# A mixture-of-experts stage: one expert goes from 128 slots with split weights to 64 slots with whole weights

## The chip, the cores and the metric

The kernel runs on one core of a Trainium2 chip. The metric is the device time of one launch in microseconds. The kernel before took 2102.27 us (median of three runs, 2098.06 to 2103.82).

## The reference

A two-layer model on 256 latent tokens and 256 context tokens, width 1024, float32. Layer 0 has neighbourhood attention, a state-space scan and a dense feed-forward; layer 1 has window attention and retention, and then, for the 256 latent tokens alone, a mixture of experts:

```
logits = h @ router                       # 256 x 8
top 2 experts of each token, softmax over the two -> gate
for e in 8 experts:                       # w1, w3: 1024 x 3584, w2: 3584 x 1024
    out += gate[:, e] * ((silu(h @ w1[e]) * (h @ w3[e])) @ w2[e])
```

The rest is `xl + g2 * out` and a last RMS norm. One expert's three matrices are 44 MB, all eight 352 MB, and each is read from HBM once. On its inputs the reference's router gives the eight experts 87, 39, 55, 145, 15, 52, 18 and 101 tokens.

## The kernel before

**Experts by rank.** Expert 0 is always position 0 (its loads start before the router is known). The other seven are sorted by their token counts into positions 1 to 7: here 145, 101, 55, 52, 39, 18 and 15 tokens. `CAPS` says how many slots each position has. Tokens are gathered into slots by a one-hot product (`gather_k`), and the outputs are scattered back by another (`comb` in `finish`). An expert with more tokens than slots would get a further whole pass in the `For_i` loop at the end (L1900).

**Two ways to multiply.** A *split* expert has 128 slots. Each weight tile (128 x 2048 float32, 1 MB) is split by ScalarE and VectorE into a high and a low float32r part (`split2`, L269 and L270); TensorE does three passes (L1554 to L1556) with all 128 columns of the array. A *whole* expert has 64 slots and uses the float32 tile as it is (`mmb`, L1551, and `stage_b`, L1763): the products of even and odd blocks stand side by side in the two 64-column halves of the array, and their partial sums are added later. Such a product shows as two records in the trace. Positions 0, 2 and 3 are split; 4 to 7 are whole; position 1 (192 slots) is split, with one block of 128 slots and one of 64 (L1558 and L1559, two passes).

**Chunks and their order.** Each expert is worked in 7 chunks of 512 hidden units. A chunk has 6 weight tiles: four of w1 and w3 (`stage_a`) and two of w2 (`stage_b`). The list `jobs` (L1447) sets the order: 7 chunks of position 0, 7 of 2, 7 of 3, then 28 of positions 4 to 7 with the 7 chunks of position 1 set between them. In the loop at L1867 `stage_a` of a chunk comes before `stage_b` of the chunk before; in the middle of `stage_a` the hidden values of the chunk before are transposed (`stage_t`). At each tile of `stage_a` one piece of waiting work is done (`fill`): a gather for a later expert (8 for each `prep_` call) or a `comb` of an expert that has ended (4 each).

**Weight tiles.** All weight DMAs go through SyncE's queue in the order of `plan`. Raw, high and low tiles share one tag of 11 buffers (`wtile`, NWT). `next_w` hands out the next tile; `prime` keeps 5 raw tiles fetched beyond those handed over and splits one tile ahead (AHEAD = 1). The tile framework places the instructions in its own order by priority, so a DMA can be issued as soon as a buffer is free.

**Sums.** The outputs of an expert are accumulated over its 7 chunks in the two PSUM banks of tag "mm". Position 1 cannot have these: its chunks go to banks of "ax" and "pt" and are added to `ysp` in SBUF by VectorE (L1858, L1860). `ysp` lies in the context half of `xT`, which nothing needs any more.

Of the kernel before, what the change touches and what calls it, by code (L numbers as in the profile page):

```python
# [10 lines left out]
F32 = mybir.dt.float32  # L11
# [7 lines left out]
P = 128  # L19
D = 1024  # L20
KD = 8
# [44 lines left out]
    return arrs, where  # L66


CAPS = (128, 192, 128, 128, 64, 64, 64, 64)
_CT, _CW = _const_tables()  # L70


# [95 lines left out]
def tile_backbone(ctx: ExitStack, tc: tile.TileContext, A, out, upto=99, dbg=None):  # L168
# [8 lines left out]
    AHEAD, LEAD, NWT, PRE, SPL = 1, 4, 11, (1, 3, 5, 7), (1, 3)  # L177
    LEADS = (6, 6, 6, 6, 5)
# [17 lines left out]
    def bank(tag="mm"):  # L196
        if turn and tag == "ax":
            turn.append(turn.pop(0))
            tag = turn[0]
        return ps[0].tile([P, 512], F32, tag=tag, name="bk_" + tag, bufs=NB[tag])  # L200
# [1199 lines left out]
            self.xt = xt  # L1400

    wpool, idx = [], []
    plan, loaded, ready, lead = [], [], [], [-1]

    def wtile(dt):
        return wpool[0].tile([P, 2048], dt, tag="w", name="w", bufs=NWT)
# [1 line left out]
    def load2(src, whole, parts=1):  # L1408
        raw = wtile(F32)
        dst, src = [a.rearrange("p (a b c) -> p a b c", a=2, b=parts) for a in (raw, src)]  # L1410
        for i in range(parts):
            nc.sync.dma_start(dst[:, :, i, :], src[:, :, i, :])
        return raw, whole
# [9 lines left out]
    def fetch():  # L1423
        loaded.append(plan.pop(0)())

    def prime():
        lead[0] += 1
        n = LEADS[min(lead[0], len(LEADS) - 1)]
        while plan and len(loaded) < n:
            fetch()  # L1430
        ready.append(split2(*loaded.pop(0), SPC if lead[0] < NSPC else 2048))

    def next_w():
        while len(ready) <= AHEAD and (loaded or plan):
            prime()
        return ready.pop(0)

    def w_dyn(r):
        return ((lambda c, i: A["m13"][bass.ds(r, 1), c, i].rearrange("o p k -> (o p) k")),
# [6 lines left out]

    jobs = []  # L1447
    job = 0
    for p in (0, 2, 3, 4, 5, 6, 7):
        for c in range(7):  # L1450
            jobs.append((p, c))
            if p >= 4:
                if job in (1, 5, 9, 13, 17, 20, 23):
                    jobs.append((1, sum(j[0] == 1 for j in jobs)))
                job += 1
    ws = {}

    def w_get(p):
        if p not in ws:
            ws[p] = w_of(p)  # L1460
        return ws[p]

    for n in range(len(jobs) + 1):
        if n < len(jobs):
            for i in range(4):
                plan.append(lambda p=jobs[n][0], c=jobs[n][1], i=i: load2(w_get(p)[0](c, i), p >= 4))
        if n:
            for q in range(2):
                plan.append(lambda p=jobs[n - 1][0], c=jobs[n - 1][1], q=q, n=n: load2(w_get(p)[1](c, q), p >= 4,
                                                                                 2 if n == len(jobs) else 1))  # L1470

    def moe(mp, dw, oh0):
        iota, iotd, rank8 = C("iota"), C("iotd"), C("rank8")
# [34 lines left out]
        def xg128():  # L1508
            return Pair(mp.tile([P, 2, KD, P], F32R, tag="xg", name="xg", bufs=4))
# [161 lines left out]
        def prep(specs, blocks, later):  # L1671
            oh = mk_oh(specs)
            ohT = mk_ohT(oh, specs)
            for k in range(KD):
                if later:
                    fills.append(lambda k=k: gather_k(oh, blocks, k))
                else:
                    gather_k(oh, blocks, k)
            return ohT
# [121 lines left out]
        def finish(src, gi, ohT, last=False):  # L1801
            for half in range(2):
                yh = mp.tile([P, 512], F32R, tag="yh", name="yh", bufs=2)
                yl = mp.tile([P, 512], F32R, tag="yl", name="yl", bufs=2)
                yhv, ylv = (yh, yl) if len(src[half].shape) == 2 else (two(yh), two(yl))
                S.activation(yhv, src[half], AF.Copy, scale=gsl[:, gi:gi + 1])
                V.scalar_tensor_tensor(ylv, src[half], gsl[:, gi:gi + 1], yhv.bitcast(F32),
                                       op0=ALU.mult, op1=ALU.subtract)

                def comb(m, yh=yh, yl=yl, half=half):  # L1810
                    pt = bank("ax" if last else "ada")
                    for i in range(2):
                        ms = slice((2 * m + i) * P, (2 * m + i + 1) * P)
                        o = pt[:, i * 256:i * 256 + 256]
                        T.matmul(o, yh[:, ms], ohT, start=True, stop=False)
                        T.matmul(o, yl[:, ms], ohT, start=False, stop=True)
                    for i in range(2):
                        resid(1, 5, 4 * half + 2 * m + i, pt[:, i * 256:i * 256 + 256], 1)
                        if last:
                            closing(4 * half + 2 * m + i)  # L1820

                for m in range(2):
                    fills.append(lambda m=m, comb=comb: comb(m))

        def spec(p, base=0.0, gi=None, io=iota):
            return (io, col(slp, p), base, col(gtp, p), p if gi is None else gi)


        def prep_b():
            xs[2], xs[3] = xg128(), xg128()  # L1830
            ohTs[2], ohTs[3] = prep([spec(2), spec(3)], [xs[2], xs[3]], True)

        def prep_c(a):
            t = mp.tile([P, 2, KD, 64], F32, tag="xg", name="xf", bufs=4)
# [8 lines left out]
        main = {}  # L1843

        def stage_2(p, c, gT):
            if p != 1:
                if c == 0:
                    main[p] = [[bank(), bank()]]
                stage_b(gT, main[p], c == 0, c == 6)
                if c == 6:  # L1850
                    finish(main[p][0], p, ohTs[p], p == 7)
                return
            acc = [[bank("ax"), bank("ax")] for _ in range(2)]
            stage_b(gT, acc, True, True)
            for b in range(2):
                for half in range(2):
                    if c == 0:
                        V.tensor_copy(ysp[b][half], two(acc[b][half]))  # L1858
                    else:
                        V.tensor_tensor(ysp[b][half], ysp[b][half], two(acc[b][half]), op=ALU.add)  # L1860
            if c == 6:
                finish(ysp[0], 1, ohTs[1])
                finish(ysp[1], 8, ohTs[8])

        prev = None
        gT = []
        for p, c in jobs:  # L1867
            if (p, c) == (0, 1):
                ohTs[0], = mk_ohT(oh0, [spec(0)])
                prep_b()  # L1870
            if (p, c) == (2, 1):
                prep_c(4)
            if (p, c) == (2, 3):
                prep_d()
            if (p, c) == (3, 1):
                prep_c(6)

            def mid():
                if prev is not None:
                    gT.append(stage_t(prev[1]))  # L1880

            gl = stage_a1(*a0) if prev is None else stage_a([xs[1], xs[8]] if p == 1 else [xs[p]], mid)
            if prev is not None:
                stage_2(*prev[0], gT.pop())
            prev = ((p, c), gl)
# [95 lines left out]
```

## Time and profile before

| | |
|---|---|
| Runs, median (range) | 2102.27 us (2098.06 to 2103.82) |
| Profiled execution | 2096.44 us, span 2094.7 us |
| PE / PEld / DVE / ACT busy | 97% / 69% / 61% / 43% of the span |
| Mean granted TensorE clock | 0.993 |
| Read from HBM | 493.40 MB, 236 GB/s over the span |

The busy time of PE is that of pipelined records whose ends are modelled. DMA is the mean busy share of the 16 DMA engines, GB/s what they moved. The experts begin at about half of the span, where GB/s rises above 300.

### The profile page before, as it was taken

To read this page: it belongs to the slowest core of one execution; us is meant where nothing else is said; L and a number is where in the kernel's file an instruction comes from. 1 tells how busy PE (TensorE), PEld (TensorE's weight loads), DVE (VectorE), ACT (ScalarE), POOL (GpSimd) and SP (SyncE) were. 2 spreads that over 40 slices of the span, in tenths; PEclk is the share of its full clock that TensorE was granted. 3 is DMA by queue.
4 is the path that set the end of the run, shared out by engine and by line. 5 is a ranking of instruction groups with operands and counts; after the bars stand their busy time and mean duration, and the time that the engine had idled before them with its cause. 6 is when DMAs were issued, how large, how long until landed. Compare 5 with 4: busy or idle time off the path is not lost. (4 is left out here: it accounts for less than half of the span.)

```text
span 2094.7 us, 26701 instructions
## 1 busy us (share of the span) xinstructions
PE 2026.0 (97%) x10170; PEld 1438.0 (69%) x10170; DVE 1288.0 (61%) x1878; ACT 906.0 (43%) x1296; POOL 109.1 (5%) x148
## 2 busy tenths in 40 slices
PE   7999999889999999999999999999999999999997
PEld 4776756688777878888888888878654554545453
DVE  5366557777566664765477888887644344434443
ACT  4346525643222223544356776767532232232322
POOL 0000015600000000100101000000000000000000
PEclk9999999999999999999999999999999999999998
DMA  8422432025444674322254999999989999999994
GB/s 317 150 94 96 151 121 95 24 68 161 142 150 151 209 236 128 125 61 81 84 228 146 337 364 323 322 334 335 371 352 397 401 406 398 390 418 383 384 361 181
DMA packets 89445, 496.25 MB, mean 237 GB/s; under 512 B 10080, under 2 KB 10848, under 8 KB 46048
## 3 DMA queue, kind: packets, MB, share of 16 engines
q1 hardware_dynamic: 89312, 494.49, 64.3%
q8 instruction: 82, 1.34, 0.3%
q14 instruction: 51, 0.42, 0.1%
HBM read 493.40 MB, written 1.05 MB: 236 GB/s over the span
## 5 line engine op out<-in xcount | busy, mean ns | idle before, releaser
L270 DVE TENSOR_TENSOR w<-w 128x2048 fp32r<-128x2048 f32 (+1 forms) x186 | 384.5, 2081 | 58.7 <-ACT w L269 40.9
L269 ACT ACTIVATE w<-w 128x2048 fp32r<-128x2048 f32 (+1 forms) x186 | 320.5, 1748 | 62.2 <-DVE w L270 35.4
L269 ACT ACTIVATE whi<-raw 128x1024 fp32r<-128x1024 f32 x151 | 160.0, 1060 | 404.1 <-PE bk_mm L298 263.3
L270 DVE TENSOR_TENSOR wlo<-raw,whi 128x1024 fp32r<-128x1024 f32 x151 | 186.6, 1236 | 140.8 <-ACT whi L269 138.3
L297 PE MATMUL bk_mm<-fH,whi 128*128 128x512 f32 (+1 forms) x360 | 140.0, 390 | 2.0 <-DVE xT L518 1.2
L299 PE MATMUL bk_mm<-fH,wlo 128*128 128x512 f32 (+1 forms) x360 | 138.8, 387 | 2.1 <-DVE wlo L270 2.1
L297 PE MATMUL bk_mm<-hH,whi 128*128 128x512 f32 (+1 forms) x384 | 137.5, 361 | 2.2 <-ACT hH L269 2.2
L298 PE MATMUL bk_mm<-fL,whi 128*128 128x512 f32 (+1 forms) x360 | 139.2, 388 | 0.0
L298 PE MATMUL bk_mm<-hL,whi 128*128 128x512 f32 (+1 forms) x384 | 136.2, 355 | 0.0
L299 PE MATMUL bk_mm<-hH,wlo 128*128 128x512 f32 (+1 forms) x384 | 135.5, 354 | 0.0
L1551 PE MATMUL bk_pt<-w,xf 128*64 128x512 f32 x448 | 113.0, 601 | 0.0
L1704 ACT COPY g<-bk_ax 64x512 f32<-64x512 f32 x35 | 20.4, 582 | 207.9 <-PE bk_ax L1551 207.7
L1551 PE MATMUL bk_ax<-w,xf 128*64 128x512 f32 x448 | 107.2, 597 | 0.0
L1763 PE MATMUL bk_mm<-w,gf 128*64 128x512 f32 x448 | 105.3, 597 | 0.0
L1555 PE MATMUL bk_ax<-w,xg 128*128 128x512 f32 x224 | 90.6, 405 | 7.2 <-DVE w L270 7.2
L1554 PE MATMUL bk_ax<-w,xg 128*128 128x512 f32 x224 | 89.6, 400 | 0.0
L1555 PE MATMUL bk_pt<-w,xg 128*128 128x512 f32 x220 | 88.5, 402 | 0.4 <-DVE w L270 0.2
L1556 PE MATMUL bk_ax<-w,xg 128*128 128x512 f32 x224 | 88.8, 396 | 0.0
L456 POOL TENSOR_TENSOR rstd<-rstd,mhalf 128x2 f32<-128x2 f32 (+2 forms) x11 | 10.3, 937 | 1496.1 <-DVE rstd L455 1477.0
L1554 PE MATMUL bk_pt<-w,xg 128*128 128x512 f32 x220 | 88.2, 401 | 0.0
L1556 PE MATMUL bk_pt<-w,xg 128*128 128x512 f32 x220 | 87.5, 398 | 0.0
L297 PEld LDWEIGHTS bk_mm<-hH,whi 128*128 128x128 f32 x384 | 71.8, 188 | 21.8 <-issue 5.4
(568 smaller groups left out, 4357.4 us busy)
## 6 DMA issues: line engine op xcount, KB each, us to landing
w<-in_m SPq DMA_DIRECT2D x334, 1024.0 KB, 7.6
raw<-in_f SPq DMA_DIRECT2D x66, 512.0 KB, 3.7
araw<-in_adc SPq DMA_DIRECT2D x56, 512.0 KB, 3.9
araw<-in_ada SPq DMA_DIRECT2D x32, 512.0 KB, 7.2
raw<-in_evx SPq DMA_DIRECT2D x29, 512.0 KB, 3.7
raw<-in_odx SPq DMA_DIRECT2D x22, 512.0 KB, 3.6
raw<-in_evo SPq DMA_DIRECT2D x12, 512.0 KB, 3.7
xT<-in_xt SPq DMA_DIRECT2D x4, 1024.0 KB, 6.4
```

The lines of the kernel that those rows point to most:

```text
L269: a = S.activation(hi, src, AF.Copy)
L270: v = V.tensor_tensor(lo, src, hi.bitcast(F32), op=ALU.subtract)
L297: T.matmul(o, wh, xh, start=first, stop=False)
L298: T.matmul(o, wh, xl, start=False, stop=False)
L299: T.matmul(o, wl, xh, start=False, stop=last)
L456: G.tensor_tensor(r, r, mhalf[:, :n], op=ALU.pow)
L1551: T.matmul(o[c:c + 64], sl(b[0]), wh, start=k < 2, stop=k >= K - 2, tile_position=(0, c))
L1554: T.matmul(o, sl(b[0]), wh, start=first, stop=False)
L1555: T.matmul(o, sl(b[0]), wl, start=False, stop=False)
L1556: T.matmul(o, sl(b[1]), wh, start=False, stop=last)
L1704: S.copy(g[0:64], hb[b][0][64:128])
L1763: T.matmul(accs[0][half][64 * q2:64 * q2 + 64], gT[0][0][:, f, :], wh[:, hs], start=first and q == 0, stop=last and q == 1, tile_position= ...
```

## The change

`CAPS` gives position 3 64 slots. It becomes a whole expert: its gathered tokens are one float32 tile of 64 slots, and its weights are not split. Its chunks alternate with those of position 2. As both need sums at once, position 3 takes the way of position 1: PSUM banks of "ax" and "pt", and sums in `ysp[0]`. `finish` of 2 and 3 then comes after the 14 chunks, and the gathers for positions 6 and 7 (`prep_c(6)`) are asked for at chunk 1 of position 4. `next_w` now primes up to four tiles as long as no split tile is among them, and `prime` fetches more as long as a count of the buffers in use (`room`) leaves space.

```diff
-CAPS = (128, 192, 128, 128, 64, 64, 64, 64)
+CAPS = (128, 192, 128, 64, 64, 64, 64, 64)
...
+    def room():
+        cost = [1 if w[1] is None else 2 for w in ready + used] + [1] * len(loaded)
+        return NWT - sum(cost) - (0 if not loaded or loaded[0][1] else 2)
+
     def prime():
         lead[0] += 1
         n = LEADS[min(lead[0], len(LEADS) - 1)]
-        while plan and len(loaded) < n:
+        while plan and (len(loaded) < n or lead[0] >= len(LEADS) and room() > 0):
             fetch()
...
     def next_w():
-        while len(ready) <= AHEAD and (loaded or plan):
+        while (len(ready) <= AHEAD or len(ready) < 4 and not any(w[1] is not None for w in ready)) and (loaded or plan):
             prime()
-        return ready.pop(0)
+        used.append(ready.pop(0))
+        del used[:-1]
+        return used[0]
...
-    for p in (0, 2, 3, 4, 5, 6, 7):
+    for p in (0, 2, 4, 5, 6, 7):
         for c in range(7):
             jobs.append((p, c))
+            if p == 2:
+                jobs.append((3, c))
...
-                plan.append(lambda ...: load2(w_get(p)[0](c, i), p >= 4))
+                plan.append(lambda ...: load2(w_get(p)[0](c, i), p >= 3))
...
         def prep_b():
-            xs[2], xs[3] = xg128(), xg128()
-            ohTs[2], ohTs[3] = prep([spec(2), spec(3)], [xs[2], xs[3]], True)
+            xs[2], xs[3] = xg128(), [mp.tile([P, KD, 64], F32, tag="xg", name="xf", bufs=4)]
+            ohTs[2], ohTs[3] = prep([spec(2), spec(3, io=iotd)], [xs[2], xs[3]], True)
...
         def stage_2(p, c, gT):
-            if p != 1:
+            if p not in (1, 3):
...
-            acc = [[bank("ax"), bank("ax")] for _ in range(2)]
+            acc = [[bank("ax"), bank("ax")] for _ in gT]
             stage_b(gT, acc, True, True)
-            for b in range(2):
+            for b in range(len(gT)):
...
             if c == 6:
-                finish(ysp[0], 1, ohTs[1])
-                finish(ysp[1], 8, ohTs[8])
+                for b in range(len(gT)):
+                    finish(ysp[b], (p, 8)[b], ohTs[(p, 8)[b]])
...
-            if (p, c) == (3, 1):
+            if (p, c) == (4, 1):
                 prep_c(6)
```

## Rows read from the trace of the kernel before

**Rows 1.** The page's 40 slices of the span: tenths busy, and GB/s.

```profile
PE   7999999889999999999999999999999999999997
PEclk9999999999999999999999999999999999999998
DMA  8422432025444674322254999999989999999994
GB/s 317 150 94 96 151 121 95 24 68 161 142 150 151 209 236 128 125 61 81 84 228 146 337 364 323 322 334 335 371 352 397 401 406 398 390 418 383 384 361 181
```

**Rows 2.** Windows of two stages: length, busy us (records) by engine, clock, DMA share, GB/s.

```profile
core 0: us, PE busy (x) PEld busy (x) DVE busy (x) ACT busy (x) POOL busy (x), PEclk, DMA share, GB/s
1249.40:1494.85 245.45, 243.90 (x1141) 198.52 (x1140) 207.83 (x151) 173.90 (x157) 0.00 (x0) 1.00 0.94 334
1550.17:1862.90 312.73, 305.15 (x1377) 154.38 (x1376) 127.70 (x149) 89.79 (x101) 0.00 (x0) 1.00 0.98 400
```

**Rows 3.** Timeline of ACT: L1700, once in each split chunk (start, length, engine, line).

```profile
1232.10 0.60 ACT L1700 ACTIVATE g<-bk_ax 128x512 f32<-128x512 f32 x1 [1.27 <-PE bk_ax L1556]
1249.40 0.60 ACT L1700 ACTIVATE g<-bk_ax 128x512 f32<-128x512 f32 x1 [1.27 <-PE bk_ax L1556]
...
1494.85 0.60 ACT L1700 ACTIVATE g<-bk_ax 128x512 f32<-128x512 f32 x1 [1.27 <-PE bk_ax L1556]
...
1550.17 0.60 ACT L1700 ACTIVATE g<-bk_ax 128x512 f32<-128x512 f32 x1 [2.29 <-PE bk_ax L1556]
...
1862.90 0.60 ACT L1700 ACTIVATE g<-bk_ax 128x512 f32<-128x512 f32 x1 [2.30 <-PE bk_ax L1556]
```

**Rows 4.** The weight DMA's line, 1230 to 1240 us: issues, and time to landing.

```profile
L1412 SPq DMA_DIRECT2D w<-in_m x3: 333/333/338, 1232.1 to 1237.7; - x3
...
DMA to landing us min/median/max: 4.9/5.1/5.7
```

**Rows 5.** The same line, 1600 to 1640 us.

```profile
L1412 SPq DMA_DIRECT2D w<-in_m x14: 332/333/333, 1600.1 to 1637.4; - x14
...
DMA to landing us min/median/max: 6.6/11.7/18.0
```

**Rows 6.** Windows of 10 us, columns as in rows 2.

```profile
1110.00:1120.00 10.00, 8.59 (x46) 7.00 (x47) 9.33 (x27) 3.34 (x11) 2.83 (x3) 0.85 0.31 105
...
1770.00:1780.00 10.00, 9.23 (x43) 5.12 (x40) 8.30 (x6) 6.33 (x4) 0.00 (x0) 1.00 1.01 418
```

**Rows 7.** Timeline of ACT: L1704, once in each whole chunk.

```profile
1586.99 0.58 ACT L1704 COPY g<-bk_ax 64x512 f32<-64x512 f32 x1 [12.01 <-PE bk_ax L1551]
1597.83 0.58 ACT L1704 COPY g<-bk_ax 64x512 f32<-64x512 f32 x1 [6.28 <-PE bk_ax L1551]
```

**Rows 8.** Timeline of PE between those two: a run of whole products.

```profile
1590.74 3.60 PE L1763 MATMUL bk_mm<-w,gf 128*64 128x512 f32 x16
```

**Rows 9.** Timeline near the end: the last weight DMAs, and PE beside them.

```profile
2041.88 12.73 SPq L1412 DMA_DIRECT2D w<-in_m  x8
...
2053.89 1.94 PE L1551 MATMUL bk_pt<-w,xf 128*64 128x512 f32 x8
```

**Rows 10.** Groups by form, 1150 to 2095 us: busy us, mean ns, idle before.

```profile
L270 DVE TENSOR_TENSOR w<-w 128x2048 fp32r<-128x2048 f32 x159 | 362.3, 2288 | 58.5 <-ACT w L269 40.7 <-PE bk_ax L1555 8.7 <-PE bk_pt L1555 4.2
L269 ACT ACTIVATE w<-w 128x2048 fp32r<-128x2048 f32 x157 | 298.1, 1914 | 58.6 <-DVE w L270 31.8 <-PE bk_ax L1559 16.3 <-DMA w<-in_m 5.6
```

**Rows 11.** The line of the sums in SBUF, and who waited for it (us, times).

```profile
L1860 DVE TENSOR_TENSOR xT<-xT,bk_ax x12: 678/683/690, 1658.8 to 2029.7; 128x512 f32<-128x512 f32 x12
...
  PEld bk_ax L1551: 2.2, 6
```

**Rows 12.** Waits of SyncE's queue, whole span: us in total, times, longest.

```profile
SPq L1445 <- DVE rsm L1634: 8.8, 1, 8.8
```

**Rows 13.** Waits of PE, 1500 to 2050 us: us in total, times, longest.

```profile
PE bk_ax L1555 <- DVE w L270: 10.9, 12, 2.1
```

More of the change, by code (lines that the diff above doesn't have):

```diff
@@ L1402, in tile_backbone @@
     wpool, idx = [], []
-    plan, loaded, ready, lead = [], [], [], [-1]
+    plan, loaded, ready, used, lead = [], [], [], [], [-1]
     def wtile(dt):
@@ L1465, in tile_backbone @@
             for i in range(4):
-                plan.append(lambda p=jobs[n][0], c=jobs[n][1], i=i: load2(w_get(p)[0](c, i), p >= 4))
+                plan.append(lambda p=jobs[n][0], c=jobs[n][1], i=i: load2(w_get(p)[0](c, i), p >= 3))
         if n:
             for q in range(2):
-                plan.append(lambda p=jobs[n - 1][0], c=jobs[n - 1][1], q=q, n=n: load2(w_get(p)[1](c, q), p >= 4,
+                plan.append(lambda p=jobs[n - 1][0], c=jobs[n - 1][1], q=q, n=n: load2(w_get(p)[1](c, q), p >= 3,
                                                                                  2 if n == len(jobs) else 1))
```

## The prediction

> **What bounds the kernel now.** I began with the slices of the page [rows 1]: PE is full nearly everywhere at the full clock, so that alone says little; what tells the stages apart is GB/s, 320 to 370 in slices 23 to 28 and about 400 from slice 31 on. All of the change lies there, so I took two stretches by their windows [rows 2]: that of positions 2 and 3, where PE is busy 243.9 of 245.45 us at 334 GB/s, and four rounds of the later stage (four whole chunks and one of position 1 each), 305.15 of 312.73 us at 400 GB/s. Both are full on PE, but the DMA engines too show 0.94 and 0.98. Which of the two is the bound needs the price of a chunk. The timeline of ACT has one L1700 for each split chunk [rows 3]: without fills 1249.40 - 1232.10 = 17.30 us, and from there to 1494.85 us 13 chunks in 245.45 us, so 245.45 - 13 x 17.30 = 20.55 us for the 32 fills in this stretch (4 of `finish(0)`, 8 of `prep_c(4)`, 8 of `prep_d`, 4 of `finish(2)`, 8 of `prep_c(6)`): 0.64 us each. A chunk's 6 tiles are 6.29 MB; in 17.30 us that is 364 GB/s. Is that the most the DMAs can do? A DMA is issued there every 2.8 us and lands after 5.1 [rows 4], so hardly two are in flight. In the later stage up to 18.0 us pass from issue to landing [rows 5], a queue of seven, and a 10 us window moves 418 GB/s while DVE is busy for 8.30 us [rows 6]. So I read the split stage as bound by PE, its DMAs as waiting for buffers, and 420 GB/s (2.50 us a tile) as the ceiling.
>
> By the Trainium skill's page "DMA: Bandwidth & Descriptors" (section Measured) a transfer of 1 MB gets 341 GB/s, and only far larger ones come near 425; by that the split stage would be DMA bound already, and a pair of chunks would take 12.58 MB / 341 GB/s = 36.9 us, a gain of next to nothing. The trace disagrees: the same 1 MB transfers run at 418 GB/s in [rows 6], since several are in flight.
>
> **The change part by part.** *A whole chunk in place of a split one.* Two L1704 with nothing but whole products between them stand 1597.83 - 1586.99 = 10.84 us apart [rows 7], which is three runs of 16 records at 3.60 us [rows 8]. A pair (split and whole) then needs 17.30 + 10.84 = 28.14 us of PE. 20 of the 32 fills stay in this stage: 20 x 0.64 / 7 = 1.83 us a pair, together 29.97 us. Its 12 tiles need 12 x 2.50 = 29.96 us of DMA. So PE and DMA come out level, and neither hides the other's hitches. How much such a level stage loses is seen later: a round there has 30 tiles (74.9 us at the ceiling) and takes (1862.90 - 1550.17) / 4 = 78.2 us [rows 3], 4.4% more. I take the same: 31.3 us a pair, 219 us for seven. Now the 14 chunks take 14 x 17.30 + 20.55 = 262.8 us. Gain 43.8 us; bounds: no loss at all, 7 x 29.97 = 209.8 us (gain 53.0), and a whole run that goes at the pace of the DMAs, 17.30 + 6 x 2.50 + 1.83 = 34.1 us a pair (gain 24).
>
> *Why the buffers let it through.* The stream alternates six split and six whole tiles. In the six whole ones PE uses 6 tiles in 10.84 us while 4.3 land; in the six split ones it uses 6 in 17.3 us while 6.9 land. The store of landed tiles must swing by less than two. The 11 buffers hold 6 tiles beyond the one in use among split tiles (by the code 5 fetched and one primed; high and low parts take two buffers each) and 10 among whole ones: when the last DMAs go out at 2054.6 us PE is in the w3 tiles of the last chunk but one, with 10 tiles left [rows 9]. This also means that the framework uses all 11 buffers already, so I give the extra fetches of `room` nothing.
>
> *The splits that go.* 42 tiles less to split: 42 x 2.29 = 96 us of DVE and 42 x 1.91 = 80 us of ACT [rows 10]. PE hides both now, so they gain nothing by themselves, but they leave DVE room for the new work: two additions of 0.68 us per chunk [rows 11], 9.6 us in all, hidden beside products. What may show is a wait for a PSUM bank that such an addition still reads: position 1 has it 6 times for 2.2 us [rows 11], 0.37 us each, so 7 x 0.37 = 2.6 us; bounds 0 and 2.6, and I take the upper since the same banks turn faster here. Behind that waiting weight load PE itself is queued, so it counts in full.
>
> *Fills and queues that move.* `finish(2)` and the gathers of `prep_c(6)` now come in the later stage: 12 x 0.64 = 7.7 us of PE there, where PE is 97.6% busy [rows 2], so I count it in full; at best the DMA-bound moments hide it (0). On SyncE's queue the number of DMAs is unchanged; position 3's index is read into a register seven chunks earlier. That line waits once, 8.8 us, before all these [rows 12], and DMAs are issued 6 tiles ahead: nothing.
>
> *Earlier priming of splits.* Where PE passes from whole to split tiles it now waits for the low part, 12 times, 10.9 us [rows 13]. Priming up to four tiles starts that split up to three whole tiles (5.4 us) sooner, if the tile has landed by then; I take half, 5.4 us; bounds 0 and 10.9. What then is late next is the landing itself.
>
> *Sum:* -43.8 + 2.6 + 7.7 - 5.4 = -38.9 us. Against the profiled execution, 2096.4 us, that is 2057.5. The median of the runs is 5.8 us above the profiled one, so I predict 2102.3 - 38.9 = 2063 us.
>
> **The rivals.**
> (a) *The DMAs are the bound beside splitting.* For: their share is 0.94 at 334 GB/s in the split stage [rows 2], as if there were little left; a chunk without fills takes 364 GB/s. Against: 418 GB/s with DVE at 83% [rows 6]. At 364 GB/s a pair takes 34.6 us, 242 us for seven, a gain of 20.8: 2102.3 - 20.8 + 4.9 = 2086 us; at 334 GB/s 37.7 us a pair and 2108 us. The page's 341 GB/s for 1 MB would lie between them.
> (b) *Everything overlaps.* For: the store of tiles needs to swing by less than two. Gain 53.0, no bank wait, all of the 10.9 us saved, fills in full: 2102.3 - 53.0 - 10.9 + 7.7 = 2046 us. Against: the 4.4% that the later stage loses already.
> (c) *Slower: a gap at each turn from whole to split tiles that lets the clock fall.* If the store is empty at the end of a whole run, the first split tile lands late and then still needs 1.91 + 2.29 us on ACT and DVE [rows 10] before its first full use. With the landing that is 4.2 + 2.5 = 6.7 us of idle PE in each pair. At an idle stretch the granted clock does fall: 0.85 as the mean of a window with 8.59 us busy [rows 6], which is 3 us at 1.2 GHz instead of 2.4, and costs 1.5 us of work. 29.97 + 6.7 + 1.5 = 38.2 us a pair, 267.2 us: 4.4 slower there, and with the bank waits and fills (10.3) 2102.3 + 14.7 = 2117 us. It decides from a gap of (262.8 - 10.3) / 7 - 29.97 = 6.1 us a pair on, clock included. Against: the present turns cost 0.9 us each [rows 13] at a full clock. The Trainium skill's page "TensorE: Matmul & The Clock Gate" (section Why this matters for your kernels) likewise warns of gaps between bursts of matmuls that halve the clock; the trace agrees in that window.
> (d) *The change doesn't do what it says:* position 3 has more than 64 tokens, and the overflow loop makes a whole split pass, 7 x 17.30 = 121 us, some 2185 us in all. The reference's router gives it 55.
>
> **How the numbers follow.** Forecast 0.60 (2063; its own bounds 2050 to 2078), (a) 0.20, (b) 0.12, (c) 0.07, (d) 0.01. The range 2042 to 2092 takes in (b) and the nearer part of (a) and leaves out the rest. A measurement tells about 0.3%, 6 us, from no change: faster 0.60 + 0.12 + 0.18 = 0.90, same 0.02 from (a) and 0.01 from (c), slower 0.06 + 0.01.
>
> **What would show it.** L1556's split chunks and L1551's whole ones alternating from about 1250 us; seven pairs in 215 to 225 us, at 395 to 405 GB/s, DMA share near 1 and a full clock; 42 fewer records of L269 and L270 on weight tiles; about 1 us or less of PE wait at each turn; the rounds of the later stage still 77 to 80 us. Pairs of 34 us at some 365 GB/s would speak for (a), gaps of several us with a falling clock for (c). The prediction is wrong if the 14 chunks don't get at least 20 us shorter, or if the later stage changes by more than 10 us.

## The result: slower, in two stages

The changed kernel takes 2184.99 us (median of 4 runs, 2184.0 to 2191.88) against 2103.05 us for the kernel before: 1.041 times as long, 95% interval [1.0395, 1.0424]. The forecast was 2063 us. The profiled run took 2184.0 us, with a span of 2181.9 us.

The slices of the page, as in [rows 1]:

```profile
PE   7999999999999999999999998989897998989897
PEclk9999999999999999999999998999998999989998
```

PE is still nearly full, but in slices 25, 31 and 36 the clock has dents that it did not have. Position 1's chunks are the landmarks again (timeline of ACT, the one instruction in each split chunk, now L1708; the first three rows are chunks of position 2, the last two lie a round apart):

```profile
1413.14 0.60 ACT L1708 ACTIVATE g<-bk_ax 128x512 f32<-128x512 f32 x1 [0.89 <-PE bk_ax L1564]
1447.83 0.60 ACT L1708 ACTIVATE g<-bk_ax 128x512 f32<-128x512 f32 x1 [0.89 <-PE bk_ax L1564]
1483.82 0.60 ACT L1708 ACTIVATE g<-bk_ax 128x512 f32<-128x512 f32 x1 [0.90 <-PE bk_ax L1564]
...
1571.34 0.60 ACT L1708 ACTIVATE g<-bk_ax 128x512 f32<-128x512 f32 x1 [2.30 <-PE bk_ax L1564]
1660.94 0.60 ACT L1708 ACTIVATE g<-bk_ax 128x512 f32<-128x512 f32 x1 [2.29 <-PE bk_ax L1564]
```

A pair (a split chunk and a whole one) is 34.7 and 36.0 us here, 41 to 46 us where gathers are filled in; the forecast was 31.3 with the fills spread over all pairs. A round of the later stage, 1571.34 to 1660.94, is 89.6 us; before, it was 78.2 on average [rows 3]. I cut both kernels at the same events: from the first L1708 of position 2 (1245.09 us; before 1249.40) to position 1's first chunk, and from there to its last. Windows of the kernel before:

```profile
1249.40:1550.17 300.77, 296.68 (x1359) 227.37 (x1358) 238.81 (x179) 194.73 (x174) 0.00 (x0) 1.00 0.93 337
...
1550.17:1996.77 446.60, 435.30 (x1961) 224.35 (x1960) 186.35 (x215) 130.69 (x145) 0.00 (x0) 1.00 0.97 395
```

and of the changed one (columns as in [rows 2]: length, PE, PEld, DVE, ACT, POOL busy, clock, DMA share, GB/s):

```profile
1245.09:1571.34 326.25, 291.50 (x1205) 171.99 (x1204) 163.79 (x168) 122.95 (x139) 0.00 (x0) 0.91 0.78 311
...
1571.34:2080.80 509.46, 457.18 (x1961) 238.10 (x1960) 186.20 (x215) 130.82 (x144) 0.00 (x0) 0.95 0.86 346
```

The alternating stage, which was to get 43.8 us shorter, is 25.5 us longer, and the later stage, which was to stay, is 62.9 us longer. (The fills that were to cost 7.7 us in the later stage still run ahead of position 1's first chunk, so in the first of these windows; with them and the bank waits the forecast for this window is 33.5 us less.) With 3.2 us behind the last chunk and 4.3 us less ahead, that is the whole difference of the spans, 87.2 us. In the later stage the work is the same (1961 PE records in both), and the loss has two halves: PE idle rose from 446.60 - 435.30 = 11.3 us to 52.3, and the same products took 21.9 us longer, at a mean clock of 0.95 instead of 1.00. The DMA share fell from 0.97 to 0.86: the DMAs are not what binds. What PE waited for between those two chunks (us in total, times, longest), after:

```profile
PE bk_mm L1771 <- DMA w<-in_m: 31.9, 6, 7.9
PE bk_po L1746 <- DVE g L1717: 10.7, 8, 2.2
PE bk_ax L1563 <- DVE w L270: 6.0, 6, 1.1
PE bk_ax L1562 <- ACT w L269: 3.6, 2, 1.8
```

and before:

```profile
PE bk_ax L1555 <- DVE w L270: 7.9, 10, 2.0
PE bk_po L1738 <- DVE g L1709: 3.4, 7, 0.5
```

31.9 + (10.7 - 3.4) + 3.6 - (7.9 - 6.0) = 40.9 us is the rise in idle time. Its largest part is a wait that did not exist: L1771, a product with a whole w2 tile, waits for a DMA. One such place on PE:

```profile
1817.46 0.43 PE L1746 MATMUL bk_po<-ca,g 64*128 64x64 f32 x4 [0.49 <-DVE g L1717]
1817.82 1.94 PE L1771 MATMUL bk_mm<-w,gf 128*64 128x512 f32 x8
1827.69 1.94 PE L1771 MATMUL bk_mm<-w,gf 128*64 128x512 f32 x2 [7.93 <-DMA w<-in_m]
1829.56 0.80 PE L1562 MATMUL bk_ax<-w,xg 128*128 128x512 f32 x1
```

and, in the same 15 us, ACT:

```profile
1817.60 1.91 ACT L269 ACTIVATE w<-w 128x2048 fp32r<-128x2048 f32 x1 [1.72 <-DMA w<-in_m]
1820.30 1.91 ACT L269 ACTIVATE w<-w 128x2048 fp32r<-128x2048 f32 x1 [0.78 <-DMA w<-in_m]
1822.63 1.91 ACT L269 ACTIVATE w<-w 128x2048 fp32r<-128x2048 f32 x1 [0.43 <-DMA w<-in_m]
```

Three split tiles of position 1 lie there, their high parts ready from 1819.5 us on, and PE does not use them: in its order a w2 product of the chunk before stands ahead of them, whose tile comes later in the stream. Until that tile lands the split tiles give no buffer back, and the next DMAs wait for them. The weight DMA's line on SyncE's queue, between the same two chunks, after:

```profile
SPq L1412 <- DVE w L270: 128.9, 24, 11.2
```

and before:

```profile
SPq L1412 <- DVE w L270: 29.3, 16, 3.6
```

Next splits wait in turn for a buffer that PE still reads, six times, for 52.7 us (before, six times for 13.7):

```profile
ACT w L269 <- PE bk_ax L1567: 52.7, 6, 11.6
```

In the kernel before, PE passes at this turn (from whole to split products) from the last w2 product to the split ones with waits of 0.49 and 0.28 us:

```profile
1772.27 0.43 PE L1738 MATMUL bk_po<-ca,g 64*128 64x64 f32 x4 [0.49 <-DVE g L1709]
1772.63 1.94 PE L1763 MATMUL bk_mm<-w,gf 128*64 128x512 f32 x8
1774.50 0.50 PE L1554 MATMUL bk_ax<-w,xg 128*128 128x512 f32 x1
...
1775.49 0.50 PE L1555 MATMUL bk_ax<-w,xg 128*128 128x512 f32 x1 [0.28 <-DVE w L270]
```

### The profile page after: what moved, and what is told of

The parts are those of the page before. It is cut to its first block, busy times and chain, and to the rows that moved or that the text cites. A ratio compares the mean times of both kernels' runs of the same rounds, so it can differ in the third digit from the quotient of the medians.

```text
span 2181.9 us, 26264 instructions
## 1 busy us (share of the span) xinstructions
PE 2039.1 (93%) x10002; PEld 1394.4 (64%) x10002; DVE 1209.7 (55%) x1856; ACT 833.9 (38%) x1261; POOL 110.3 (5%) x148
## 5 line engine op out<-in xcount | busy, mean ns | idle before, releaser
L270 DVE TENSOR_TENSOR w<-w 128x2048 fp32r<-128x2048 f32 (+1 forms) x144 | 288.6, 2021 | 109.7 <-ACT w L269 94.1
L269 ACT ACTIVATE w<-w 128x2048 fp32r<-128x2048 f32 (+1 forms) x144 | 239.6, 1697 | 110.4 <-PE bk_ax L1567 57.6
L1771 PE MATMUL bk_mm<-w,gf 128*64 128x512 f32 x448 | 115.5, 605 | 31.9 <-DMA w<-in_m 31.9
L1559 PE MATMUL bk_ax<-w,xf 128*64 128x512 f32 x560 | 142.6, 603 | 0.0
L1559 PE MATMUL bk_pt<-w,xf 128*64 128x512 f32 x560 | 142.1, 600 | 0.0
L1771 PEld LDWEIGHTS bk_mm<-w,gf 128*64 128x64 f32 x448 | 32.7, 138 | 93.6 <-issue 63.4
L1559 PEld LDWEIGHTS bk_ax<-w,xf 128*64 128x64 f32 x560 | 41.8, 138 | 73.9 <-issue 72.1
L297 PEld LDWEIGHTS bk_mm<-fH,whi 128*128 128x128 f32 x360 | 68.0, 190 | 22.5 <-issue 3.6
L1559 PEld LDWEIGHTS bk_pt<-w,xf 128*64 128x64 f32 x560 | 39.3, 136 | 66.8 <-issue 63.6
L298 PEld LDWEIGHTS bk_mm<-hL,whi 128*128 128x128 f32 x384 | 72.2, 188 | 13.2 <-issue 3.4
L1713 DVE TENSOR_TENSOR g<-g,bk_ax 64x512 f32<-64x512 f32 x42 | 28.4, 677 | 91.6 <-ACT g L1712 91.6
```

Of the source, the lines that this page charges most:

```text
L269: a = S.activation(hi, src, AF.Copy)
L270: v = V.tensor_tensor(lo, src, hi.bitcast(F32), op=ALU.subtract)
L297: T.matmul(o, wh, xh, start=first, stop=False)
L298: T.matmul(o, wh, xl, start=False, stop=False)
L1559: T.matmul(o[c:c + 64], sl(b[0]), wh, start=k < 2, stop=k >= K - 2, tile_position=(0, c))
L1713: V.tensor_tensor(g[0:64], g[0:64], hb[b][0][0:64], op=ALU.add)
```

## The experiments

All times are medians; the kernel before took 2099 to 2101 us beside each of them.

**Which edit costs it.** The changed kernel with `prime` and `next_w` as before (`e1_old_priming`), and the kernel before with the new ones (`e2_new_priming_only`):

```
e1: -    def room(): ...
    -        while plan and (len(loaded) < n or lead[0] >= len(LEADS) and room() > 0):
    +        while plan and len(loaded) < n:
    -        while (len(ready) <= AHEAD or len(ready) < 4 and not any(...)) and (loaded or plan):
    +        while len(ready) <= AHEAD and (loaded or plan):
e2: the reverse, in the kernel before
```

> The changed kernel with prime and next_w as they were before (5 tiles fetched, one primed, no count of buffers); position 3 stays whole and alternates. Theory A (the loss comes from the priming edits, which fill the 11 buffers with raw tiles so that splits and with them DMAs wait): the 14 chunks fall from 263 to about 220 us, rounds of the later stage return from 89 to 78 us, 2063 us in all. Theory B (the loss comes from alternating a whole with a split expert and summing in SBUF, whatever the priming): about 2185 us, the later stage's rounds stay at 89 us.

> The kernel before with only the new prime and next_w; position 3 stays split, 128 slots, after position 2. Theory A: the later stage alone loses 11 us in each of its 7 rounds, about 2103 + 78 = 2180 us; the split stage, where a split tile is always primed, keeps its 17.3 us a chunk. Theory B: 2103 us, within 10.

e1: 2123.26 us, 1.0106 [1.009, 1.0123]. e2: 2171.35 us, 1.0338 [1.0317, 1.0359]. So the priming alone costs the kernel before about 71 us, and the changed one 62. In e1 the rounds are 77 to 80 us again; in e2 they are 89 to 92. Neither theory had 2123 us: the new priming makes 62 of the 122 us by which the forecast was missed. Its cost lies in the later stage alone, for e1's alternating stage is as long as that of the changed kernel (326.25 us):

```profile
1249.90:1576.22 326.32, 295.31 (x1203) 172.22 (x1202) 163.69 (x168) 122.44 (x140) 0.00 (x0) 0.91 0.79 311
```

e1 is still 23 us too slow where some 39 less were forecast. The alternation is the suspect, and e6 below tests it.

**Which half of the priming.** Without `room` but with four splits primed (`e3_no_room`), and with `room` alone (`e4_no_deep`):

```
e3: -        while plan and (len(loaded) < n or lead[0] >= len(LEADS) and room() > 0):
    +        while plan and len(loaded) < n:
e4: -        while (len(ready) <= AHEAD or len(ready) < 4 and not any(...)) and (loaded or plan):
    +        while len(ready) <= AHEAD and (loaded or plan):
```

> The changed kernel without the fetches of room (5 tiles fetched as before), but with up to four tiles primed. Within theory A: if the extra fetches do the harm, the rounds of the later stage return to 78 us and the time to about 2065; if the deep priming does it, nothing changes, about 2185 us. Theory B: 2185 us.

> The changed kernel with only one tile primed ahead as before, but with the fetches of room. Within theory A: if the deep priming does the harm, about 2065 us; if the extra fetches do it, about 2185 us. Theory B: 2185 us.

e3: 2122.4 us, 1.0105 [1.0085, 1.0125], like e1. e4: 2192.15 us, 1.0437 [1.0413, 1.0461]. `room` is all of it, about 63 us; the deep priming is worth nothing measurable. In e3's later stage no L1771 waits for a DMA; in e4's, nine do, for 24.7 us.

**Buffers, as a cause of the slow pairs.** In `e5_two_buffers` (on e1) a split tile keeps one buffer beside the raw one, not two (its low part is written over the high one, which is lost); in `e7_own_split_bufs` the split parts have buffers of their own:

```
e5: -        hi, lo = wtile(F32R), wtile(F32R)
    +        hi = wtile(F32R)
    ...
    +        lo = hi
e7: -        return wpool[0].tile([P, 2048], dt, tag="w", name="w", bufs=NWT)
    +        return wpool[0].tile([P, 2048], dt, tag="w", name="w", bufs=7)
    -        hi, lo = wtile(F32R), wtile(F32R)
    +        hi, lo = [wpool[0].tile([P, 2048], F32R, tag="whl", name="w", bufs=4) for _ in range(2)]
```

> The changed kernel with the old priming (2123 us, pairs of 37.2 us without fills), in which the low part of a split tile is written over its high part, so that a split tile needs two of the 11 buffers while it is split instead of three, and one afterwards instead of two. The instructions and their sizes stay; the products use the low part alone, so the result is not the reference's. Theory A (at each turn from whole to split tiles all buffers hold raw tiles; the split and behind it the DMAs wait for buffers, PE idles some 5 us and its clock falls): pairs of about 31 to 32 us, 2123 - 7 x 5.5 = 2085 us or less. Theory B (the turn is late by the order of the work on ACT and DVE, whatever the buffers): pairs stay at 37 us, 2123 us.

> The changed kernel with the old priming, the 11 buffers parted: 7 for raw tiles, 4 for the high and low parts, so that no DMA can take a buffer that a split needs. Theory A: the split of the first tile at each turn starts when it has landed, the PE gap at a turn falls from 5 to 2 us or less and pairs to about 33 us in the alternating stage; among whole tiles only 7 are ahead instead of 10, so the later stage may lose 1 or 2 us a round: about 2105 us. Theory B: pairs stay at 37 us, 2123 us or more.

e5: 2116.93 us, 1.0081 [1.0055, 1.0107], about 6 us better than e1, but its pairs stay at 37 us. So one buffer fewer for each split tile does not make the pairs faster; the 6 us are gained in the later stage (444.9 us against 450.6). e7: 2160.24 us, 1.0287 [1.0261, 1.0314]: four buffers for the parts are too few, a chunk that is all split takes 20.7 us instead of 17.3, and pairs 38 to 41. It says nothing for the alternation.

**The alternation, undone.** `e6_sequential` is e1 with the third expert's whole chunks behind the second's split ones:

```
-    for p in (0, 2, 4, 5, 6, 7):
+    for p in (0, 2, 3, 4, 5, 6, 7):
...
-            if p == 2:
-                jobs.append((3, c))
```

> The changed kernel with the old priming, but the seven chunks of position 3 come after the seven of position 2 and do not alternate with them; position 3 stays whole and sums in SBUF. Theory A (turns cost): one turn in place of seven; seven split chunks at 17.3 us with their fills and seven whole ones at the pace of the DMAs (15 us), about 240 us in place of 262, 2123 - 22 = 2101 us. Rival (a whole third expert with sums in SBUF costs that much wherever it stands): 2123 us.

2078.83 us, 0.9906 [0.9881, 0.993]: faster than the kernel before and the changed one, and 22 us faster than theory A had it. The same 14 chunks, the same two sums in SBUF, the same buffers. Its windows over the split chunks and over the whole ones behind them:

```profile
1250.00:1362.00 112.00, 111.31 (x534) 91.27 (x533) 95.60 (x81) 79.31 (x80) 0.00 (x0) 1.00 0.92 326
1378.40:1491.50 113.10, 101.89 (x461) 36.19 (x461) 42.32 (x66) 21.39 (x31) 0.00 (x0) 1.00 1.01 420
```

The first is bound by PE at 326 GB/s, the second by the DMAs at 420 GB/s, both at the full clock. From the first chunk of position 2 to position 1's first:

```profile
1246.40:1527.70 281.30, 262.01 (x1191) 158.12 (x1190) 162.38 (x165) 121.91 (x140) 0.00 (x0) 0.98 0.93 361
```

Against the changed kernel's 326.25 us this is 45.0 less: 291.50 - 262.01 = 29.5 us of longer products (clock 0.98 against 0.91) and 34.75 - 19.29 = 15.5 us of idle PE. By the mean clocks some 24 us of the former are the clock's, (1 - 0.91) x 326.25 - (1 - 0.98) x 281.30, an estimate. So the alternation lost more by the clock than by waiting.

**The gathers that moved.** `e8_prep_later` puts them seven chunks later still:

```
-            if (p, c) == (4, 1):
+            if (p, c) == (5, 1):
```

> The changed kernel with the old priming, the gathers for positions 6 and 7 asked for at chunk 1 of position 5 instead of 4, away from the turn into the first chunk of position 1. From the last split chunk of position 2 to the first chunk of position 1 it takes 85.7 us, some 12 more than the chunks and fills in it add up to. If the gathers in a row at that turn (1.35 us each, the split behind them on ACT) make that, about 12 us less there and 2111 us; if they only fill a gap that is there anyway, 2123 us.

2119.04 us, 1.0091 [1.0059, 1.0123]. That is 4 us below e1, but the intervals overlap, so no gain is shown. The stage before position 1 gets shorter (its first chunk at 1557.5 us instead of 1576.2), and a later round gets 90.7 us long (79.9 in e1). The cost goes where the gathers go.

**Fetches, other ways.** `e9_two_buffers_lead8` is e5 with the old rule and more fetches, `e14_room_reserve` is e4 with two buffers always kept free:

```
e9:  -    LEADS = (6, 6, 6, 6, 5)
     +    LEADS = (6, 6, 6, 6, 8)
e14: -        return NWT - sum(cost) - (0 if not loaded or loaded[0][1] else 2)
     +        return NWT - sum(cost) - 2
```

> As the run with two buffers a split tile (alternating, old priming, low part over high part, result not the reference's; 2117 us, pairs of 37 us), but with 8 raw tiles fetched ahead in place of 5; the buffers suffice for that here. Theory C (among split tiles only 5 tiles are on their way, so the whole tiles that follow eat this store, the DMAs have not refilled it when the next split tile is wanted, and buffers alone did not help because the fetches were not asked for): pairs fall to 32 us or less, 2117 - 7 x 5 = 2082 us. Theory B (the splits come late by the order of the work on ACT and DVE): pairs stay at 37 us, 2117 us.

> The changed kernel with one tile primed ahead and the fetches of room (2192 us), but room always keeps two buffers free, not only when the next fetched tile is a split one. Theory D (among whole tiles room fills all buffers with raw tiles before a split tile comes up, so that its high and low parts wait until PE has used up whole tiles, each split waits for the one before, and the DMAs wait for the raw tile behind the split): two free buffers let the first split start, most of the harm goes, about 2123 to 2140 us. Rival (more fetches in the program do harm as such, by the order that the framework gives the queue): 2185 us or more.

e9: 2195.06 us, 1.0454 [1.0422, 1.0485]. e14: 2198.49 us, 1.047 [1.0441, 1.0499]. Theory C falls, since e9's pairs stay at 37 us, and D's two free buffers do not cure the loss. But these runs do not show that buffers play no part. In e9 the chunks of position 0, split ones alone, take 22.2 us instead of 17.3, and there splits wait for a buffer that PE still reads (1167.83 to 1279.37 us; with the other two banks 44.1 us):

```profile
ACT w L269 <- PE bk_ax L1559: 15.9, 9, 2.0
```

That makes some 30 of its 78 us against e5; 44 are lost in the later stage. And the reserve of e14 is a count in the program: on the chip six splits of its later stage wait for a buffer all the same, and six L1771 wait for a DMA, 28.0 us in all:

```profile
ACT w L269 <- PE bk_mm L1771: 58.3, 6, 12.0
```

What holds the buffer in e14 is a w2 product that PE has not done, which left PE's order as a suspect.

**The order on TensorE.** The extra fetches come earlier in the program and so change the order in which the framework puts instructions on each engine. `e15_after_ordered` keeps the changed kernel's fetches and only ties that order: `stage_2`, with the w2 products, behind the last w1 or w3 product of the chunk that runs beside it. `e16_old_priming_ordered` is the same edit on e1:

```
+                            tail[0] = mmb(hb[b][i], blk, ...)   # mmb returns its last product
...
-                stage_2(*prev[0], gT.pop())
+                with tc.issue_after(tail[0].ins) if tail[0] is not None else ExitStack():
+                    stage_2(*prev[0], gT.pop())
```

> The changed kernel with one edge more: on TensorE each chunk's products with w2 stand behind the last product with w1 and w3 of the chunk that is computed beside them, as they did in most places of the kernel before. Its fetches, its buffers and its alternation are those of the changed kernel. Theory O (order): the extra fetches harm because the order on TensorE lets a whole w2 product stand ahead of split products that are already there, so TensorE waits for a DMA that waits for the buffers of the split tiles. Then the waits of L1771 for a DMA (6 of them, 31.9 us in the later stage of the changed kernel) are gone, the rounds of the later stage return from 88 to 92 to 77 to 81 us, and the time is about 2120 us (2110 to 2130), that of the changed kernel with the old fetches. Rival F (fetches as such): more fetches ahead of a split tile delay it whatever TensorE's order; the rounds stay at 88 to 92 and the time at 2180 to 2200 us.

> The alternating kernel with the old fetches (2123 us), with the same edge on TensorE. If the place of w2's products also makes the gaps at each turn of the alternating stage, its pairs fall from 37.3 us towards 31.3 and the time to 2090 to 2105 us. If the gaps are the latency of the turn itself (gating of the chunk before on ACT and DVE, then the split, then the products at half clock), nothing changes, the pairs stay at 37 us and the time at 2118 to 2128 us. I hold the second for likelier.

e15: 2150.32 us, 1.0231 [1.0188, 1.0274], half way. The waits for a DMA are gone, and the rounds are 80.2, 84.3, 80.5 and 83.9 us; but the last two, 74.3 and 75.1 us in the changed kernel, stay at 73.3 and 75.4, where e16 has 65.6 and 68.2. So the order of w2 makes some 35 us of the 62, and the other 27 have another cause. The waits of splits for PE fall from 52.7 to 17.4 us, with the same fetches. Like for like the rest is larger: against e16, which has the same edge without `room`, e15 loses 40 us, 29 of them in the later stage. From position 1's first chunk to its last (window and PE waits of e15):

```profile
1573.92:2051.43 477.51, 452.03 (x1961) 237.43 (x1960) 185.84 (x215) 130.69 (x145) 0.00 (x0) 0.96 0.92 370
```

```profile
PE bk_ax L1563 <- DVE w L270: 11.1, 12, 2.1
PE bk_po L1748 <- DVE g L1719: 10.7, 8, 2.2
PE bk_ax L1562 <- ACT w L269: 3.6, 2, 1.8
```

Idle is 25.5 us, 14.2 more than before, but the products take 16.7 us longer, at a clock of 0.96. A turn in e15, on PE:

```profile
1927.31 0.43 PE L1748 MATMUL bk_po<-ca,g 64*128 64x64 f32 x4 [2.19 <-DVE g L1719]
...
1929.93 0.80 PE L1563 MATMUL bk_ax<-w,gh 128*128 128x512 f32 x1 [1.06 <-DVE w L270]
1930.52 0.63 PE L1564 MATMUL bk_ax<-w,gl 128*128 128x512 f32 x1
1930.95 0.63 PE L1563 MATMUL bk_pt<-w,gh 128*128 128x512 f32 x1
...
1936.32 0.40 PE L1567 MATMUL bk_pt<-w,gh 128*128 128x512 f32 x1
1936.56 0.40 PE L1562 MATMUL bk_ax<-w,gh 128*128 128x512 f32 x1
```

and on ACT:

```profile
1925.15 0.58 ACT L1717 COPY g<-bk_pt 64x512 f32<-64x512 f32 x1 [2.33 <-PE bk_pt L1559]
1925.64 3.71 ACT L269 ACTIVATE w<-w 128x2048 fp32r<-128x2048 f32 x2
```

ACT sits idle for 2.33 us, copies a part of the hidden values of the chunk before (g, its gate), and only then splits. PE waits 2.19 us for that gate and 1.06 us for the low part, and behind the two gaps its products come every 0.43 us instead of every 0.23 until 1936.3 us, the half clock (0.52 granted from 1929.9 to 1936.3 us). In e16 the split of the tile stands ahead of the gate's copy on ACT, PE waits 0.98 us at the same turn, and the mean clock of its later stage is 1.00:

```profile
1894.55 1.90 ACT L269 ACTIVATE w<-w 128x2048 fp32r<-128x2048 f32 x1
1896.99 0.58 ACT L1711 COPY g<-bk_pt 64x512 f32<-64x512 f32 x1 [0.54 <-PE bk_pt L1553]
...
1898.83 0.50 PE L1557 MATMUL bk_ax<-w,gh 128*128 128x512 f32 x1 [0.98 <-DVE w L270]
```

e16: 2110.27 us, 1.0051 [1.0034, 1.0067], 13 us better than e1 where I held no change for likelier. Its pairs are 35 to 36 us. One of them, window and the waits in it on PE:

```profile
1403.55:1439.51 35.96, 31.70 (x129) 19.49 (x128) 18.73 (x15) 14.27 (x11) 0.00 (x0) 0.91 0.89 350
```

```profile
1422.53 0.43 PE L1742 MATMUL bk_po<-ca,g 64*128 64x64 f32 x4 [2.20 <-DVE g L1713]
...
1425.68 0.79 PE L1557 MATMUL bk_mm<-w,gh 128*128 128x512 f32 x1 [2.05 <-DVE w L270]
```

It is the same kind of turn: 2.20 us for the gate and 2.05 for the low part, 35.96 - 31.70 = 4.3 us idle in all, and 31.70 - 28.14 = 3.6 us of products at half the clock. 28.14 + 4.3 + 3.6 is the pair. In e1 it is 4.3 and 4.8, and on ACT both splits (1433.63 us) stand behind the copy of the gate (1433.14 us), as in e15:

```profile
1416.00:1453.20 37.20, 32.94 (x129) 19.18 (x128) 18.76 (x15) 14.30 (x12) 0.00 (x0) 0.91 0.86 339
```

**Fewer turns.** `e18_three_turns` is e16 with the whole chunks in blocks of 2, 2 and 3:

```
-            if p == 2:
-                jobs.append((3, c))
+            if p == 2 and c in (1, 3, 6):
+                for d in {1: (0, 1), 3: (2, 3), 6: (4, 5, 6)}[c]:
+                    jobs.append((3, d))
```

> The alternating kernel with the old fetches and the edge on TensorE (2110.3 us), with the third expert's seven whole chunks put behind the split ones in blocks of 2, 2 and 3 instead of singly: three turns from whole to split chunks become two inside the stage where there were six, and the work is the same. Theory G (gap and clock): what a pair costs above its two chunks (34.9 to 36.0 us against 17.3 + 10.84 = 28.1) is paid at each turn from a whole to a split chunk, as a wait of TensorE of about 3.8 us and a half clock behind it that costs 3 us; but two whole chunks in a row are bound by their DMAs and take about 15 us each instead of 11, which takes back some 3 us for each chunk that is not alone. Net some 3 to 4 us for each of four turns fewer, 2094 to 2102 us, and the mean clock of the stage up from 0.90. Rival (the whole weights as such, or the fills moved to that stage, not the turns): 2107 to 2114 us.

2099.37 us, 0.9991 [0.9978, 1.0005]: 10.9 us less for four turns fewer, in the range expected. Its stage against e16's:

```profile
1246.87:1549.20 302.33, 280.26 (x1191) 163.97 (x1190) 161.67 (x165) 121.75 (x139) 0.00 (x0) 0.94 0.86 335
```

```profile
1246.82:1560.31 313.49, 282.49 (x1203) 170.09 (x1202) 163.63 (x168) 122.37 (x139) 0.00 (x0) 0.92 0.82 324
```

With one turn in the stage (e6, without the edge) it is 281.3 us, with three 302.3, with seven 313.5. The loss goes with the turns, though not in proportion; why three turns still cost 21 us was not taken apart.

**The best version.** `e12_spread` is e1 in sequence, with the third expert's output in PSUM as before and position 1's split chunks spread over 35 whole ones; `e17_spread_ordered` adds the edge on PE:

```
-    for p in (0, 2, 4, 5, 6, 7):
+    for p in (0, 2, 3, 4, 5, 6, 7):
...
+            if p >= 3:
+                if job in (1, 6, 11, 16, 21, 25, 29):
...
-            if p not in (1, 3):
+            if p != 1:
```

> Position 3 whole, after position 2 and not alternating, old priming; its sums go to the mm banks as those of positions 4 to 7 do, and the 7 chunks of position 1 are spread over the 35 whole chunks of positions 3 to 7 in place of the 28 of 4 to 7. From the sequential run (2079 us), in which the whole chunks of position 3 run at the ceiling of 420 GB/s with PE idle and the later stage has PE full at 399 GB/s: if both limits can be shared out like that, seven rounds of 36 tiles at 2.5 us and some 2% on top, 92 us each, and about 2055 to 2062 us. If a turn costs as much as it saves, 2079 us.

> The kernel with whole chunks for the third-largest expert, none of them alternating, the split chunks of the second half spread over 35 whole ones (2076.7 us), with the same edge on TensorE. If a turn from whole to split chunks loses time to the order on TensorE there too, the time falls by some us for each of 7 turns, to 2050 to 2070 us; if that stage is bound by its DMAs and by the products, it stays within 0.3% of 2076.7 us (2070 to 2083).

e12: 2076.74 us, 0.9884 [0.986, 0.9908], 1.2% under the kernel before and 5% under the changed one. It missed its 2055 to 2062. e17: 2078.53 us, 0.9894 [0.9867, 0.9921]. Neither can be told from e6. In e12's later stage PE is busy for 520 of 545 us and the DMAs move 393 GB/s at a share of 0.97:

```profile
1422.06:1967.05 544.99, 519.99 (x2333) 257.29 (x2332) 206.80 (x252) 146.84 (x181) 0.00 (x0) 0.98 0.97 393
```

Both are nearly full there, which would explain why it matters little where position 1's chunks stand among the whole ones. PE's order in the first round of this stage is the same in e12 and e17, so there the edge has nothing to give.

## Why the prediction was wrong

*Right.* The bound of each stage: the split stage on PE, with its DMAs waiting for buffers, and 420 GB/s as the ceiling; e6's whole stage runs at 420. The price of a whole chunk (a pair of e1 and e16 is 28.14 us, the gaps and the clock) and the fewer splits (126 tiles instead of 168). That the change does what it says; no overflow pass ran, so rival (d) is out. The bank waits stayed small: a weight load of the changed kernel waited once for an addition in SBUF, 0.8 us.

*The step that failed first: "I give the extra fetches of `room` nothing".* They cost about 62 us (e1 and e3 against the changed kernel), half of the miss of 122 us, all of it in the later stage. I took a fetch for a matter of buffers, and reasoned that the framework uses all of them anyway. Buffers are a link of the chain, as the waits of the splits show, but more room for them did not cure it (e14), and an edge on the order of PE, with the same fetches, took 35 us of it away (e15). With the fetches earlier in the program, the order on the engines changed. On PE, w2 products came to stand ahead of split products that were ready. On ACT the split came to stand behind the gate's copy of the chunk before, and PE got a gap of 3 us at a turn, with a half clock behind it; that accounts for the idle and the clock of e15's later stage. That it is ACT's order which makes the rest (27 us against e1, 40 against e16) is read from the traces; no run changed that order alone, so this part of the cause stays open.

*The second: "31.3 us a pair", with "Why the buffers let it through" behind it.* A pair measured 34.7 to 37.3 us without fills, and this makes the other half of the miss. The account was kept in tiles landed against tiles used. For all that is lost it took the 4.4% of a stage with one turn in five chunks, and held a turn at the 0.9 us that it cost before [rows 13]. But before, a chunk that turned had whole products of its neighbours left to run beside the split. Where split and whole chunks alternate singly, the gate of the whole chunk goes over ACT and DVE to PE and the next split over ACT and DVE behind it, one after the other, and PE has nothing else: 4.3 us idle. And the clock then falls: 3.6 to 4.8 us more. That is rival (c), given 0.07, in its effect and not in its cause: it had the first split tile landing late, but in e1's pairs without fills (1378.74 to 1490.51 us) no split waits for a DMA. Its gap of 6.7 us with 1.5 us of clock was too long in the one and too short in the other, for the sum it named 38.2 us a pair with fills; without fills, 36.4 against the 37.2 of e1. Its turning point, a gap of 6.1 us a pair, clock included, was passed: 4.3 + 4.8 = 9.1 us. That its 2117 us lies near e1's 2123 is luck in part, since its cause and the sizes of its two terms were off; that the changed kernel's 2185 us is the figure of rival (d) is luck altogether.

A rule and a number can agree by accident here. The Trainium skill's page "DMA: Bandwidth & Descriptors" (section Measured) has 341 GB/s for transfers of 1 MB; the prediction worked out 36.9 us a pair by it and set it aside. e1's pair takes 37.2 us at 339 GB/s. Yet the same transfers run at 420 GB/s in e6, and e18 and e16 change the time by order and turns alone; so the DMAs did not bind (their share in e1's pair is 0.86), and rival (a) is out although its figure looks right. What bore on the pairs is the Trainium skill's page "TensorE: Matmul & The Clock Gate" (section Why this matters for your kernels), which warns of gaps between bursts of matmuls: the trace agrees that the clock falls behind gaps, here two short ones of 2.20 and 2.05 us: 0.91 over a pair with 4.3 us idle, against 1.00 in e6's windows of split and of whole chunks.

*The others.* The 7.7 us for fills: in the changed kernel they stayed ahead of position 1's first chunk. Where the gathers do lie in the later stage they cost more than 0.64 us each: e8's longer round is 90.7 us instead of 79.9, 10.8 us for eight gathers. The 5.4 us for the earlier priming: nothing (e3 against e1). That the splits that go give no time by themselves was not tested apart.

*Where the gain was.* 42 splits less and 7 x (17.30 - 10.84) = 45 us less of PE work are worth 20 us when the chunks follow one another, where the forecast was 39: whole chunks in a row are bound by their DMAs; in e6's window at 420 GB/s eight of them take 113.1 us, 14.1 each with their fills, instead of 10.84. Alternating was to win that back and lost 45 us against it.

## What to carry to other kernels

When two kinds of work alternate so that each hides the other's limit, price the turn, not only the two means: follow the last result of one kind through every engine to the first product of the next, add what the clock takes behind the gap, and multiply by the number of turns. An earlier fetch is not free because buffers are: where a framework orders the engines by the program, it can move instructions on all of them, so compare the order on PE and ACT at a turn, and look in the changed profile for a wait that did not exist before. When a loss is left, change one of count, place or order at a time; here the count of turns and one edge on one engine told more than four kernels on buffers and fetches.

## What the runs showed of the hardware

Behind two gaps of PE at a turn, 2.19 and 1.06 us, products went on at the lower of the two levels, 1.2 GHz, for some 6 us (0.43 us a product instead of 0.23; 0.52 granted in e15 from 1929.9 to 1936.3 us); behind 0.49 and 0.28 us at a turn of the kernel before, the granted clock stayed at 1.00 (1772 to 1782 us), 2.4 GHz. In the changed kernel longer products cost 29.5 us against 15.5 of waiting in the alternating stage, in comparison with e6, and 21.9 against 41.0 in the later stage, in comparison with the kernel before. DMAs of 1 MB held 420 GB/s over 113 us (e6), at a share of 1.01.
